# Border of stages in a two-layer trunk: the last chunk's residual by column tiles, squares summed on VectorE, the shift as two more moving columns

## The chip, the cores and the metric

One core of a Trainium2 chip (trn2). The metric is the device time of one execution in microseconds; lower is better. Engines are named as in the profile: PE is TensorE (PEld its weight loads), DVE VectorE, ACT ScalarE, POOL GpSimd, SP the engine that issues most DMAs.

## The reference

A sequence of 256 frames of width 2048 goes through two layers. Each layer is norm, mixer, residual, then norm, MLP, residual; the norm is modulated by vectors made from `c`:

```python
for layer in range(DEPTH):
    mod = jnp.einsum('bd,de->be', c_act, mod_w[layer]) + mod_b[layer]
    sh1, sc1, g1, sh2, sc2, g2 = [m[:, None, :] for m in jnp.split(mod, 6, axis=-1)]
    h = rms_norm(x, norm_mix_w[layer]) * (1.0 + sc1) + sh1
    mix = gdn_attn_mixer(h, w_in) if layer == 0 else mamba2_ssd(h, w_in)
    x = x + g1 * mix
    h = rms_norm(x, norm_mlp_w[layer]) * (1.0 + sc2) + sh2
    x = x + g2 * sq_relu_mlp(h, mlp_w1[layer], mlp_w2[layer])
```

What matters here is one step: from the last product of a stage over the residual, the mean of squares over 2048 features and its inverse root to the first product of the next stage.

## The kernel before

**Layout.** `x` lies transposed, features on partitions: four tiles of 128 x 4 x 256 (`self.x`, L1542). Weights stream in as chunks of 1 MB. `loader` (L473) DMAs a chunk to `raw`, and for each half makes `wh` (a rounded copy on ACT, L317) and `wl` (the rest, on DVE, L321), so that products of the reduced-precision float type reach full accuracy: high by high, high by low, low by high. Activations are pairs too: a unit holds high and low halves side by side, so that `wh` multiplies both in one matmul of 512 moving columns, and `wl` the high half in one of 256. There are four buffers each of `wh` and `wl`, and a new split waits until the matmuls have left its buffer.

**Order.** A framework that tracks tiles sets the waits, and a scheduler the order on each engine; some instructions are pinned (`keep_in_program_order`). Work is queued in Python: `emit` (L241) runs a chunk's matmuls after the next chunk's load was issued; small steps wait in `fast` and `bg` and are taken between matmuls.

**A stage's end.** A chunk of the output products (`c_item`, L565) has two column tiles of 128 features, ct 0 and ct 1, in one PSUM tile `pw` of 128 x 2 x 2 x 256. The last chunk (`cb` 7) runs "tile" by tile: ct 0's matmuls (low weights, then high), then ct 1's (high, then low). Afterwards `residual` (L918) adds the gated result to `x`: for each f (ct 0 and ct 1 of that chunk) two DVE operations at L925. There are three borders at which a norm follows: mixer to MLP in layer 0, layer 0 to layer 1, mixer to MLP in layer 1. At the kernel's end `residual` is followed by the output's DMAs.

**The norm's start.** `sumsq` (L809) squares `x` on ACT. Up to the third tile of `x` (`cb` < 3) the squares are added into `ss` on DVE (L833); for the last tile they, and `ss`, are summed over partitions by TensorE with a column of ones into `pm` (L823). `norm_r` (L837) makes the inverse root by Newton's method on DVE (`nv`, `rsy`, `rsn`, `rst`); `norm_bc` (L843) spreads it over the partitions with two transposes; `norm_unit` (L849) multiplies (`hf`, L862), rounds to the high half on ACT (L864) and takes the low half on DVE (L865).

**The early chunk.** To give TensorE work in the meantime, one chunk of the next stage is multiplied by the first eight features' tiles of `x` with the modulation's scale, before the root is known: `early_units` (L707) prepares units `xs`, `early_item` (L726) multiplies. The root is applied later to the product (`terms`, L733), and the shift's share comes in by 16 matmuls of the same weights with `sh` (two columns, high and low; L768) into a third PSUM tile, transposed back in `terms` (L741 to L745: `er`, `ee`, `eb`). `early_add` (L777) adds it where the next stage's first half is finished. `norm` (L872) runs the early chunk step by step among the norm's instructions, and `first_blocks` (L786) starts the next stage's first two chunks as units arrive.

Of the kernel before, what the change touches and what calls it, by code (L numbers as in the profile page):

```python
# [18 lines left out]
P = 128  # L19
# [93 lines left out]
class Trunk:  # L113
# [39 lines left out]
    def unit(self, dt=F32, shape=None):  # L153
        return self.u_p.tile(shape or [P, 4, SEQ], dt, tag="u", name=self.nm("u"))
# [410 lines left out]
    def c_item(self, ps, src, act, first, last, after=None, order="kind"):  # L565
# [5 lines left out]
        def run():  # L571
# [39 lines left out]
    def c_blocks(self, w, cbs, acts, then, r0=0, tail=False):  # L611
# [9 lines left out]
        for r in range(2):  # L621
            for cb in cbs:
                after = (lambda cb=cb: then(ps[cb], cb)) if r else None
                self.c_item((lambda cb=cb: get(cb)), w[r0 + r, cb], (lambda n, r=r: acts(4 * r + n)), r == 0, r == 1, after,
                            "tile" if tail and r else "kind")
# [61 lines left out]
    def out_blocks(self, w, acts, r0, sink, tail=True):  # L687
# [11 lines left out]
        for m, (cb, r) in enumerate(seq):  # L699
            if m == len(seq) - self.nstill0:  # L700
                self.still = self.nstill0
            after = (lambda cb=cb: sink(ps.pop(cb), cb)) if r else None
            self.c_item((lambda cb=cb: get(cb)), w[r0 + r, cb], (lambda n, r=r: acts(4 * r + n)), r == 0, r == 1, after,
                        "tile" if tail and m == len(seq) - 1 else "kind")


    def early_units(self, key):  # L707
# [6 lines left out]
        self.sh = sh = self.s_p.tile([P, 8, 2], F32R, tag="sm", name=self.nm("sh"), bufs=32)  # L714
        self.split(shift[:, :8], sh[:, :, 0], sh[:, :, 1])
        for n in range(4):
            u = self.unit(F32R, [P, 2, 2, SEQ])
            for f in range(2):
                k = 2 * n + f
                x = self.x[k // 4][:, k % 4]  # L720
                nc.scalar.activation(u[:, f, 0], x, AF.Copy, scale=scale[:, k : k + 1])
                nc.vector.scalar_tensor_tensor(u[:, f, 1], x, scale[:, k : k + 1], u[:, f, 0].bitcast(F32), op0=ALU.mult, op1=ALU.subtract)
            xs.append(u)
            yield

    def early_item(self, src):  # L726
# [4 lines left out]
        self.early = res = {}  # L731

        def terms():  # L733
            rows = self.s2([P, SEQ], tag="er")
            nc.scalar.copy(rows[:2], res["b"][:2, :SEQ])
# [4 lines left out]
            yield  # L740
            ps = self.pm([P, 2, SEQ])[:, 0, :4]  # L741
            for ct in range(2):
                self.tr(ps[:, 2 * ct : 2 * ct + 2], rows[:2, ct * P : ct * P + P], 2)
            bias = self.small(4, "eb")
            nc.scalar.copy(bias, ps)  # L745
            nc.vector.tensor_tensor(bias[:, :2], bias[:, 0:4:2], bias[:, 1:4:2], op=ALU.add)
            yield
            nc.vector.tensor_tensor(e, e, self.row(self.R, 2), op=ALU.mult)
            return e, bias

        def run():
            while self.etask and not self.etask.done:
                self.etask.step()
            xs = self.xs
            halves = self.tiles(ws, 256)
            res["b"] = b = self.pm([P, 512])
            for hf in range(2):
                for k2 in (0, 2):
                    for k in (k2, k2 + 1):
                        u = xs[2 * hf + k // 2][:, k % 2]  # L760
                        for ct in range(2):
                            self.mmx(res["p"][ct].rearrange("p a t -> p (a t)"), halves[hf][0][:, k, ct * P : ct * P + P], u.rearrange("p a t -> p (a t)"), hf == k == 0, False)
                        for ct in range(2):
# [5 lines left out]
                yield  # L769
# [5 lines left out]
        res["p"] = [self.pm([P, 2, SEQ]) for _ in range(2)]  # L775
# [33 lines left out]
    def sumsq(self, cb, b, late=False):  # L809


        sq = self.s2([P, 2, SEQ], tag="sq")
        x = self.x[cb][:, 2 * b : 2 * b + 2]
        if cb == 3:
            if b == 0:
                self.ps_r = self.pm([P, 512])[:, :2]
            for f in range(2):
                self.nc.scalar.activation(sq[:, f], x[:, f], AF.Square)

            def sums():  # L820
                for n, a in enumerate((() if b else (self.ss,)) + (sq[:, 0], sq[:, 1])):
                    for t in range(2):
                        self.mmx(self.ps_r[:, t : t + 1], a[:, t * P : t * P + P], self.ones[:, :1], b == n == t == 0, b == n == t == 1)  # L823
# [5 lines left out]
            return  # L829
        self.nc.scalar.activation(sq, x, AF.Square)  # L830
        for f in range(2):
            if not cb == b == f == 0:
                self.nc.vector.tensor_tensor(self.ss, sq[:, 0] if cb == b == 0 else self.ss, sq[:, f], op=ALU.add)  # L833
# [38 lines left out]
    def norm(self, key, srcs):  # L872
# [15 lines left out]
        next(run)  # L888
# [29 lines left out]
    def residual(self, ps, cb, key, last, final=False):  # L918
# [4 lines left out]
        for f in range(2):  # L923
# [4 lines left out]
        if last and not final:  # L928
            self.sumsq(cb // 2, b, cb == 7)
# [559 lines left out]
    def mlp(self, layer, acts, after=None):  # L1489
# [20 lines left out]
        for f in range(NF):  # L1510
# [11 lines left out]
            for cb in range(8):  # L1522
                if f == NF - 1 and cb == 6:
                    self.still = 4
                self.c_blocks(w2, (cb,), lambda n, a=a: a[n].finish(),
                              lambda ps, cb, f=f: self.residual(ps, cb, ("mlp", layer), f == NF - 1, layer == 1 and f == NF - 1), f * 2,
# [285 lines left out]
```

## Time and profile before

| | us |
|---|---|
| median of 3 runs | 2716.48 (2715.31 to 2716.92) |
| profiled execution: span (the page gives no other time for it) | 2717.6 |
| PE busy | 2665.0 (98%) |
| PEld busy | 2350.4 (86%) |
| DVE busy | 2147.6 (79%) |
| ACT busy | 1351.2 (50%) |

The span runs from the first to the last instruction. A line of the page gives a group's place in the code, engine, operation, tiles written and read, count, busy time, mean length of one in ns, and the idle time of its engine ahead of it with what ended it. A row of the timeline has start, length, engine, line, operation and count, and in brackets the idle time just before. A row of the chain of waits has start, length and what ran. A row of the windows has a stretch, its length, the busy time and count of PE, PEld, DVE, ACT and POOL, the granted TensorE clock, the share of the DMA engines and GB/s. Matmuls overlap, so their lengths are longer than the distance from one to the next.

### The profile page before, as it was taken

The numbers are of one execution on the slowest core, as the hardware profiler recorded it, in microseconds if no ns is written. First come the engines' busy times: TensorE is split into PE (matmuls) and PEld (weight loads), VectorE is DVE, ScalarE is ACT, GpSimd is POOL, SyncE is SP. The second block draws the span as 40 slices with busy tenths as digits, with TensorE's granted clock in tenths as the row PEclk, the third lists the DMA queues.
The fourth block names the chain that finished last, engine by engine and source line by source line (L and its number), as shares of the span: only waits on it lengthen the run. The fifth ranks groups of instructions, "written<-read, shape, count | busy, mean of one in ns | idle before, by whom it ended". The sixth has DMA issues, their size and how long they took to land.

```text
span 2717.6 us, 39677 instructions
## 1 busy us (share of the span) xinstructions
PE 2665.0 (98%) x15664; PEld 2350.4 (86%) x15664; DVE 2147.6 (79%) x3081; ACT 1351.2 (50%) x1976; POOL 24.5 (1%) x98
## 2 busy tenths in 40 slices
PE   5999999999999999999999999999999999999999
PEld 5887989888888888888888888888888888888888
DVE  7998998987888888889889876897777855555554
ACT  3444454546445354454556544665555354454452
POOL 1000000000000000000000000000000000000000
PEclk9999999999999999999999999999999999999999
DMA  9986487867899898988456665554558855555554
GB/s 341 353 325 235 172 301 272 294 241 282 322 339 328 328 336 330 333 331 307 165 185 217 217 234 200 203 185 172 196 177 293 324 201 188 188 191 193 186 192 134
DMA packets 100459, 680.06 MB, mean 250 GB/s; under 512 B 11185, under 2 KB 14513, under 8 KB 19377
## 3 DMA queue, kind: packets, MB, share of 16 engines
q1 hardware_dynamic: 95376, 669.07, 68.5%
q10 hardware_dynamic: 4896, 8.46, 1.0%
q8 instruction: 123, 2.02, 0.3%
q14 instruction: 64, 0.52, 0.1%
HBM read 675.33 MB, written 2.16 MB: 249 GB/s over the span
## 4 chain that ended last, share of the span: by engine, by line
PE 90%; DVE 6%; DMA 1%; ACT 1%; issue 1%; SPq 0%; ACTq 0%; DVEq 0%
PE pw L308 70%; PE pg L308 13%; PE pm L311 4%; PE pm L308 3%; DVE mraw L439 2%; DVE wl L321 1%; PE pm L314 1%; DMA mraw<-in_mod_dram 1%; DVE u L1592 0%; ACT wh L317 0%; DVE hf L862 0%; ACT pm L1042 0%; DMA raw<-in_w_ab_dram 0%; DMA x<-in_x_dram 0%; DVE u L865 0%
## 5 line engine op out<-in xcount | busy, mean ns | idle before, releaser
L317 ACT CAST wh<-raw 128x1024 fp32r<-128x1024 f32 x870 | 907.1, 1051 | 1031.6 <-PE pw L308 732.9
L321 DVE TENSOR_TENSOR wl<-raw,wh 128x1024 fp32r<-128x1024 f32 x870 | 1048.7, 1220 | 463.8 <-ACT wh L317 349.6
L308 PE MATMUL pw<-u,wh 128*128 128x512 f32 x5584 | 1321.6, 391 | 2.6 <-DVE pad L973 1.9
L308 PEld LDWEIGHTS pw<-u,wh 128*128 128x128 f32 x5584 | 1032.2, 188 | 208.2 <-issue 3.3
L308 PEld LDWEIGHTS pw<-u,wl 128*128 128x128 f32 x5584 | 702.3, 191 | 21.3 <-issue 2.1
L308 PE MATMUL pw<-u,wl 128*128 128x256 f32 x5584 | 714.5, 283 | 0.3 <-DVE wl L321 0.3
L439 DVE SCALAR_TENSOR_TENSOR mraw<-mraw,crow 128x2048 f32<-128x2048 f32 x192 | 438.0, 2283 | 17.8 <-DMA mraw<-in_mod_dram 17.5
L308 PE MATMUL pg<-wh,u 128*128 128x512 f32 x864 | 281.6, 397 | 0.0
L308 PEld LDWEIGHTS pg<-wh,u 128*128 128x128 f32 x864 | 161.9, 188 | 32.1 <-issue 0.5
L925 DVE SCALAR_TENSOR_TENSOR x<-pw,mod,x 128x256 f32<-128x256 f32 x352 | 161.1, 478 | 22.6 <-PE pw L308 20.3
L308 PE MATMUL pg<-wl,u 128*128 128x512 f32 x432 | 169.9, 393 | 0.7 <-DVE wl L321 0.5
L308 PE MATMUL pg<-u,wh 128*128 128x256 f32 x672 | 124.6, 285 | 0.0
L308 PEld LDWEIGHTS pg<-u,wh 128*128 128x128 f32 x672 | 105.7, 192 | 0.3
L308 PEld LDWEIGHTS pg<-wl,u 128*128 128x128 f32 x432 | 81.4, 188 | 17.6 <-DVE wl L321 2.1
L308 PE MATMUL pg<-u,wl 128*128 128x256 f32 x336 | 95.3, 284 | 0.0
L308 PE MATMUL pm<-u,wh 128*128 128x256 f32 (+1 forms) x304 | 64.6, 310 | 19.2 <-ACT wh L317 19.2
L308 PEld LDWEIGHTS pm<-u,wh 128*128 128x128 f32 x304 | 49.1, 198 | 20.3 <-ACT wh L317 20.0
L308 PEld LDWEIGHTS pg<-u,wl 128*128 128x128 f32 x336 | 64.4, 192 | 0.1
L984 DVE SCALAR_TENSOR_TENSOR u<-pad,cst,u 128x256 f32<-128x256 f32 x144 | 60.6, 477 | 3.3 <-ACT u L978 3.2
L864 ACT ACTIVATE u<-hf,mod 128x256 fp32r<-128x256 f32 x64 | 29.3, 502 | 53.0 <-DVE hf L862 53.0
L1504 ACT ACTIVATE rl<-rs 128x512 f32<-128x512 f32 x64 | 40.4, 632 | 18.9 <-DVE rs L1499 14.4
L308 PE MATMUL pm<-u,wl 128*128 128x256 f32 x176 | 46.1, 290 | 3.1 <-DVE wl L321 3.1
(299 smaller groups left out, 1580.5 us busy)
## 6 DMA issues: line engine op xcount, KB each, us to landing
raw<-in_w_dram SPq DMA_DIRECT2D x256, 1024.0 KB, 5.0
mraw<-in_mod_dram SPq DMA_DIRECT2D x192, 1024.0 KB, 6.0
raw<-in_w_ab_dram SPq DMA_DIRECT2D x56, 1024.0 KB, 5.7
raw<-in_w_ssd_dram SPq DMA_DIRECT2D x48, 1024.0 KB, 4.9
raw<-in_w_sz_dram SPq DMA_DIRECT2D x32, 1024.0 KB, 4.9
raw<-in_wo_ssd_dram SPq DMA_DIRECT2D x32, 1024.0 KB, 4.8
raw<-in_wo_ab_dram SPq DMA_DIRECT2D x16, 1024.0 KB, 5.2
sE<-sd_rowd ACTq DMA_DIRECT2D x32, 256.0 KB, 4.9
```

The costliest lines, as they stand in the source:

```text
L308: self.nc.tensor.matmul(o, a, b, start=start, stop=stop, skip_group_check=True)
L311: self.nc.tensor.matmul(o, lhsT, rhs, start=True, stop=True, skip_group_check=True)
L314: self.nc.tensor.transpose(o, a, self.ident[:k, :k])
L317: a = self.nc.scalar.copy(hi, src)
L321: b = self.nc.vector.tensor_tensor(lo, src, hi.bitcast(F32), op=ALU.subtract)
L439: x = nc.vector.scalar_tensor_tensor(raw, raw, 1.0, self.crow, op0=ALU.mult, op1=ALU.mult, accum_out=t[:, f : f + 1])
L864: nc.scalar.activation(hi, h[:, f], AF.Identity, bias=shift[:, col])
L925: nc.vector.scalar_tensor_tensor(x[:, 2 * b + f], ps[:, f, n], g[:, 2 * cb + f : 2 * cb + f + 1], x[:, 2 * b + f], op0=ALU.mult, op1=ALU.add)
L984: nc.vector.scalar_tensor_tensor(h, pad[:, f, 1 + q : 257 + q], w[:, q, j : j + 1], h, op0=ALU.mult, op1=ALU.add)
L1504: nc.scalar.activation(rl, lo, AF.Relu)
```

## The change

1. **Residual by column tiles.** In the last chunk of a stage, `residual` is called for f = 0 as soon as ct 0's matmuls are issued (a new argument `mid` of `c_item`), and for f = 1 after ct 1's. This holds for the last chunk of the kernel too.
2. **Squares on DVE.** For the last tile of `x`, the squares are added into `ss` on DVE as well, up to f = 0 of the last half; TensorE sums only `ss` and the last f's squares. The kernel's first norm goes the same way.
3. **Shift as columns.** The early units get two more columns behind the 256 of the high half, the shift's high and low part (copied on ACT); high and low half no longer lie side by side. The early matmuls become 258 (high) and 256 (low) columns instead of 512, and `wl` takes 258 instead of 256. The 16 shift matmuls, their PSUM tile and the transposes go. The two columns are copied out on ACT (`eb`), and the root multiplies the product straight from PSUM.

```diff
+    def unit_ext(self):
+        t = self.u_p.tile([P, 4 * SEQ + 4], F32R, tag="u", name=self.nm("u"))
+        cut = 2 * (SEQ + 2)
+        return t[:, :cut].rearrange("p (f t) -> p f t", f=2), t[:, cut:].rearrange("p (f t) -> p f t", f=2)
...
-    def c_item(self, ps, src, act, first, last, after=None, order="kind"):
+    def c_item(self, ps, src, act, first, last, after=None, order="kind", mid=None):
...
                         if len(cts) == 2 or hf:
                             yield
+                if cts == (0,) and mid:
+                    mid()
...
-            after = (lambda cb=cb: sink(ps.pop(cb), cb)) if r else None
+            tile = tail and m == len(seq) - 1
+            mid = (lambda cb=cb: sink(ps[cb], cb, (0,))) if tile else None
+            after = ((lambda cb=cb: sink(ps.pop(cb), cb, (1,))) if tile else (lambda cb=cb: sink(ps.pop(cb), cb))) if r else None
...
         for n in range(4):
-            u = self.unit(F32R, [P, 2, 2, SEQ])
+            hi, lo = self.unit_ext()
+            nc.scalar.copy(hi[:, :, SEQ:], sh[:, 2 * n : 2 * n + 2].bitcast(F32))
...
         def terms():
-            rows = self.s2([P, SEQ], tag="er")
-            nc.scalar.copy(rows[:2], res["b"][:2, :SEQ])
+            bias = self.small(4, "eb").rearrange("p (c n) -> p c n", c=2)
+            for ct in range(2):
+                nc.scalar.copy(bias[:, ct], res["p"][ct][:, SEQ:ext])
+            nc.vector.tensor_tensor(bias[:, :, 0], bias[:, :, 0], bias[:, :, 1], op=ALU.add)
+            yield
             e = self.s2([P, 2, SEQ], tag="ee")
             for ct in range(2):
-                nc.scalar.copy(e[:, ct], res["p"][ct][:, 1])
-                nc.vector.tensor_tensor(e[:, ct], res["p"][ct][:, 0], e[:, ct], op=ALU.add)
...
-            nc.vector.tensor_tensor(e, e, self.row(self.R, 2), op=ALU.mult)
-            return e, bias
+                nc.vector.tensor_tensor(e[:, ct], res["p"][ct][:, :SEQ], self.R, op=ALU.mult)
+            return e, bias[:, :, 0]
...
+                for k in range(4):
+                    hi, lo = (a[:, k % 2] for a in self.xs[2 * hf + k // 2])
+                    for n, w in enumerate(halves[hf]):
                         for ct in range(2):
-                            self.mmx(res["p"][ct][:, 1], halves[hf][1][:, k, ct * P : ct * P + P], u[:, 0], False, hf == 1 and k == 3)
+                            o, c = res["p"][ct], w[:, k, ct * P : ct * P + P]
+                            self.mmx(o[:, :ext], c, hi, hf == k == n == 0, hf == n == 1 and k == 3)
+                            if n == 0:
+                                self.mmx(o[:, :SEQ], c, lo, False, False)
                     yield
-                for k in range(4):
-                    for n in range(2):
-                        self.mmx(b[:2, :SEQ], self.sh[:, 4 * hf + k], halves[hf][n][:, k], hf == k == n == 0, hf == 1 and k == 3 and n == 1)
...
+        if cb < 3 or b == 0:
+            sq = self.s2([P, 2, SEQ], tag="sq")
+            nc.scalar.activation(sq, x, AF.Square)
+            for f in range(2):
+                if not cb == b == f == 0:
+                    nc.vector.tensor_tensor(self.ss, sq[:, 0] if cb == b == 0 else self.ss, sq[:, f], op=ALU.add)
+            return
+        for f in fs:
+            sq = self.s2([P, SEQ], tag="sq")
+            nc.scalar.activation(sq, x[:, f], AF.Square)
+            if f == 0:
+                nc.vector.tensor_tensor(self.ss, self.ss, sq, op=ALU.add)
+                continue
...
-        next(run)
+        for _ in range(3):
+            next(run)
         self.sums()
...
-        for f in range(2):
+        for f in fs:
             for n in range(2):
                 nc.vector.scalar_tensor_tensor(x[:, 2 * b + f], ps[:, f, n], g[:, 2 * cb + f : 2 * cb + f + 1], x[:, 2 * b + f], op0=ALU.mult, op1=ALU.add)
```

The order of TensorE at the middle border, from the end of ct 0 (`pw` is the last chunk's tile, `pm` the early chunk's, `u` an activation unit, `wh` and `wl` a weight chunk's parts; [waits X] names the engine waited for). Before:

```order
L308 MATMUL pw_11897<-u_11197,wh_11893 128x512 x2
L308 MATMUL pw_11897<-u_10902,wh_11889 128x512 x2
L308 MATMUL pw_11897<-u_11000,wh_11889 128x512 x2
L308 MATMUL pw_11897<-u_11099,wh_11893 128x512 x2
L308 MATMUL pw_11897<-u_11197,wh_11893 128x512 x2
L308 MATMUL pw_11897<-u_10902,wl_11890 128x256 x2
```

and now, from the row behind the end of ct 0:

```order
L317 MATMUL pm_11969<-u_11785,wh_11920 128x258 [waits Activation_49]
L317 MATMUL pm_11969<-u_11785,wh_11920 128x256
L317 MATMUL pm_11970<-u_11785,wh_11920 128x258
L317 MATMUL pm_11970<-u_11785,wh_11920 128x256
L317 MATMUL pm_11969<-u_11785,wl_11921 128x258 [waits DVE_49]
L317 MATMUL pm_11970<-u_11785,wl_11921 128x258
L317 MATMUL pm_11969<-u_11785,wh_11920 128x258
L317 MATMUL pm_11969<-u_11785,wh_11920 128x256
L317 MATMUL pm_11970<-u_11785,wh_11920 128x258
L317 MATMUL pm_11970<-u_11785,wh_11920 128x256
L317 MATMUL pm_11969<-u_11785,wl_11921 128x258
L317 MATMUL pw_11885<-u_10892,wh_11877 128x512 [waits DVE_49]
```

The first row of before is the end of ct 0. Before, ct 1 followed at once, without a wait; now its first matmul waits for DVE, whose residual reads the same PSUM tile, and 11 of the early chunk's 48 matmuls stand ahead of it.

The order of DVE at the same border (`x` is the residual, `pw` the last chunk, `wl` a weight split, `nv` the start of the root). Before:

```order
L321 TENSOR_TENSOR wl_11933<-raw_11930,wh_11932 128x1024 [waits DMAHW0_49,PE_49,Activation_49]
L321 TENSOR_TENSOR wl_11937<-raw_11930,wh_11936 128x1024 [waits PE_49,Activation_49]
L321 TENSOR_TENSOR wl_11984<-raw_11981,wh_11983 128x1024 [waits DMAHW1_49,PE_49,Activation_49]
L925 SCALAR_TENSOR_TENSOR x_82<-pw_11897,mod_128,x_82 128x256 [waits PE_49]
L925 SCALAR_TENSOR_TENSOR x_82<-pw_11897,mod_128,x_82 128x256 [waits DVE_49]
L925 SCALAR_TENSOR_TENSOR x_82<-pw_11897,mod_128,x_82 128x256
L925 SCALAR_TENSOR_TENSOR x_82<-pw_11897,mod_128,x_82 128x256 [waits DVE_49]
L838 TENSOR_SCALAR nv_12000<-pm_11878 128x2 [waits PE_49]
```

and now:

```order
L330 TENSOR_TENSOR wl_11921<-raw_11918,wh_11920 128x1024 [waits DMAHW0_49,PE_49]
L823 TENSOR_TENSOR ss<-ss,sq_11871 128x256 [waits DVE_49]
L330 TENSOR_TENSOR wl_11925<-raw_11918,wh_11924 128x1024 [waits PE_49,Activation_49]
L934 SCALAR_TENSOR_TENSOR x_82<-pw_11885,mod_128,x_82 128x256 [waits PE_49]
L934 SCALAR_TENSOR_TENSOR x_82<-pw_11885,mod_128,x_82 128x256 [waits DVE_49]
L829 TENSOR_TENSOR ss<-ss,sq_11946 128x256 [waits Activation_49]
L330 TENSOR_TENSOR wl_11974<-raw_11971,wh_11973 128x1024 [waits DMAHW1_49,PE_49,Activation_49]
L934 SCALAR_TENSOR_TENSOR x_82<-pw_11885,mod_128,x_82 128x256 [waits PE_49]
L934 SCALAR_TENSOR_TENSOR x_82<-pw_11885,mod_128,x_82 128x256 [waits DVE_49]
L846 TENSOR_SCALAR nv_12000<-pm_11994 128x2 [waits PE_49]
```

The residual's f = 0 half moved ahead of the weight split of the next chunk (`wl_11984`, now `wl_11974`); the f = 1 half still stands behind it. The two adds of squares are new.

More of the change, by code (lines that the diff above doesn't have):

```diff
@@ L622, in c_blocks @@
             for cb in cbs:
[L623 removed]
+                tile = tail and r == 1
+                mid = (lambda cb=cb: then(ps[cb], cb, (0,))) if tile else None
+                after = ((lambda cb=cb: then(ps[cb], cb, (1,))) if tile else (lambda cb=cb: then(ps[cb], cb))) if r else None
                 self.c_item((lambda cb=cb: get(cb)), w[r0 + r, cb], (lambda n, r=r: acts(4 * r + n)), r == 0, r == 1, after,
[L625 removed]
+                            "tile" if tile else "kind", mid)
     def n_item(self, src, acts, width, sink):
@@ L915, in norm, with residual @@
         return get
-    def residual(self, ps, cb, key, last, final=False):
+    def residual(self, ps, cb, key, last, final=False, fs=(0, 1)):
         nc = self.nc
```

61 lines of the change are left out of this document (20 added, 41 removed).

## Prediction

> **What bounds the kernel now.** I read the page first, then the stretch from the last matmul of a stage to the first of the next at the three borders, then the middle border instruction by instruction, then the kernel's two ends, then the granted clock.
>
> The page, parts 1 and 4: TensorE is busy for 98% of the span and makes 90% of the chain that ended last.
>
> ```profile
> PE 2665.0 (98%) x15664; PEld 2350.4 (86%) x15664; DVE 2147.6 (79%) x3081; ACT 1351.2 (50%) x1976; POOL 24.5 (1%) x98
> PE 90%; DVE 6%; DMA 1%; ACT 1%; issue 1%; SPq 0%; ACTq 0%; DVEq 0%
> ```
>
> So an edit pays where it takes TensorE work away, or where TensorE waits. The three borders, each from the start of the early chunk's first matmul to the first `pw` matmul of the next stage (columns: length, then busy time of PE, PEld, DVE, ACT, POOL; granted clock; DMA):
>
> ```profile
> 1301.54:1310.99 9.45, 9.02 (x60) 7.07 (x58) 7.33 (x23) 2.41 (x6) 0.00 (x0) 1.00 0.04 15
> 583.28:592.72 9.44, 9.00 (x61) 7.07 (x59) 7.34 (x23) 2.42 (x6) 0.00 (x0) 1.00 0.02 6
> 1995.76:2005.19 9.43, 8.98 (x60) 7.07 (x58) 7.33 (x23) 2.42 (x6) 0.00 (x0) 1.00 0.03 10
> ```
>
> They are alike: some 9.44 us, 9.0 of it busy. The early chunk covers the chain residual, squares, sums, rsqrt, broadcast, norm almost exactly. I work on the middle one. Its timeline (start, length, engine, line, instruction, count; idle before):
>
> ```profile
> 1296.93 3.82 PE L308 MATMUL pw<-u,wh 128*128 128x512 f32 x16
> 1300.58 1.12 PE L308 MATMUL pw<-u,wl 128*128 128x256 f32 x8
> 1301.31 1.22 DVE L321 TENSOR_TENSOR wl<-raw,wh 128x1024 fp32r<-128x1024 f32 x1 [3.69 <-ACT wh L317]
> 1301.54 0.63 PE L308 MATMUL pm<-u,wh 128*128 128x512 f32 x2
> 1302.45 1.91 DVE L925 SCALAR_TENSOR_TENSOR x<-pw,mod,x 128x256 f32<-128x256 f32 x4
> 1304.40 0.42 ACT L818 ACTIVATE sq<-x 128x256 f32<-128x256 f32 x1 [0.49 <-DVE x L925]
> 1305.56 0.50 PE L308 MATMUL pm<-ones,sq 128*128 128x1 f32 x4
> 1305.92 0.28 PE L308 MATMUL pm<-wl,sh 128*2 128x256 f32 x1
> 1306.04 0.28 PE L308 MATMUL pm<-wh,sh 128*2 128x256 f32 x1
> 1306.10 0.16 DVE L838 TENSOR_SCALAR nv<-pm 128x2 f32<-128x2 f32 x1 [1.74 <-PE pm L308]
> 1308.37 0.40 PE L314 MATMUL pm<-ident,rsy 128*128 128x128 f32 x2 [0.32 <-DVE rsy L276]
> 1310.99 1.20 PE L308 MATMUL pw<-u,wh 128*128 128x512 f32 x4
> ```
>
> Matmuls are pipelined, so their price is the step from start to start: 16 of 512 columns take 1300.58 - 1296.93 = 3.65 us, 0.229 each; 8 of 256 columns 1301.54 - 1300.58 = 0.96, 0.12 each (0.115 net, half of 0.229). The two shift matmuls are 0.12 apart.
>
> **The change part by part.** *Sums moved off TensorE.* The chain of waits shows what one ones-product with its two halves costs ahead of the last column tile:
>
> ```profile
> 1289.20 0.34 PE pm L308 x4
> 1291.70 0.34 PE pm L308 x4
> 1294.25 0.34 PE pm L308 x4
> ```
>
> Three of these go at each border; TensorE does not wait there, so this is 3 x 0.34 = 1.02 us each. The VectorE adds that replace them (0.42 us each) fall where VectorE was idle, 3.69 us ahead of 1301.31 alone.
>
> *Shift as columns.* The early chunk was 16 x 0.229 + 16 x 0.115 + 16 shift matmuls x 0.115 = 7.3 us and becomes 48 x 0.116 (16 of 256 columns, 32 of 258) = 5.6. The trace has no 258-column matmul; the nearest rows lie on one line (256 at 0.115, 512 at 0.229), so 258 should be 0.116. The saving of 1.8 us is cover, not path, unless TensorE is what ends the border. That has to be worked out.
>
> *Residual by column tiles.* Before, ct 0 ends 8 x 0.229 after 1296.93, at 1298.76, and VectorE starts at 1302.45, behind a weight split that waits for its buffer (1301.31). After, the f = 0 half starts when ct 0 drains (0.17 later), takes half of 1.91, and ends some 1.2 us after ct 0. But the order shows that the ct 1 matmuls now wait for it, and that 11 early matmuls stand ahead of them: 11 x 0.116 = 1.27 us. So TensorE loses nothing there, and ct 1 ends 1.27 us later with 37 early matmuls (4.3 us) left instead of the whole chunk.
>
> From the end of ct 1 (T): the weight split still stands ahead of the f = 1 residual, which so starts at T + 0.91 as before (1302.45 - 1301.54), takes 0.95, squares 0.42: ready at T + 2.35. The sums stand behind 19 early matmuls and the `ss` product: 19 x 0.116 + 0.34 = T + 2.54, so TensorE's queue sets them; `nv` follows 0.54 later (1306.10 - 1305.56), at T + 3.08. From `nv` to the first `pw` it was 1310.99 - 1306.10 = 4.89, made of rsqrt, broadcast, a pinned weight split, norm:
>
> ```profile
> 1308.06 0.04 DVE rsy L276
> 1308.14 1.23 DVE wl L321
> 1309.37 1.18 DVE hf L862 x3
> 1310.54 0.41 DVE u L865
> ```
>
> None of that is edited. First `pw` at T + 7.97, against 9.45 before, less 1.27 for the fill: 0.21 us gained. With the sums 1.23 us a border, 3.7 us in all. And TensorE is out of early work at about T + 5.8: it now waits 0.35 us for the broadcast and 2.1 us for the norm. The stall that was covered is late next.
>
> *The terms.* The four small copies (`er`, `ee`, `eb`) become two ahead of the norm's activations, in ACT's wait for `hf`. At the end of the first blocks TensorE waited for `er`:
>
> ```profile
> 1326.03 1.22 DVE L321 TENSOR_TENSOR wl<-raw,wh 128x1024 fp32r<-128x1024 f32 x1
> 1327.16 0.87 DVE L865 SCALAR_TENSOR_TENSOR u<-hf,mod,u 128x256 fp32r<-128x256 f32 x2
> 1327.55 0.28 PE L314 MATMUL pm<-ident,er 2*128 2x2 f32 x2 [0.61 <-ACT er L735]
> ```
>
> 0.61 + 0.21 us go, but the next matmuls in line now want the last unit's low half, done 0.45 us after 1327.16, and then a weight split that moved behind it (1.22 us). I get 0.6 + 0.2 + 0.2 us of waits for them: nothing gained, -0.4 to +0.4.
>
> *The kernel's two ends.* At the start TensorE's sums gate the first modulation products:
>
> ```profile
> 10.44 0.43 DVE ss L833
> 11.01 4.41 PE pm L308 x20
> 15.44 0.17 DVE nv L838
> 15.92 2.30 DVE mraw L439 x2
> ```
>
> 20 records at 0.22 become 8 (1.76 us) behind three more adds (3 x 0.45): 15.44 becomes 14.15, 1.3 us gained, and VectorE sets the pace from there. At the end there is no early work for the fill:
>
> ```profile
> 2712.72 1.92 DVE L925 SCALAR_TENSOR_TENSOR x<-pw,mod,x 128x256 f32<-128x256 f32 x4 [7.77 <-PE pw L308]
> ```
>
> TensorE stands 1.2 us for the f = 0 residual, and half of the 1.92 us at the end goes: 0.2 to 0.3 us lost.
>
> *The granted clock.* The new gaps have a price of their own. Here it fell in stretches of 3.41 us; the stretch before each, and one that did not fall:
>
> ```profile
> 86.60:90.01 3.41, 1.87 (x9) 1.21 (x7) 2.83 (x7) 1.32 (x2) 0.00 (x0) 1.00 0.93 320
> 90.01:93.43 3.42, 2.73 (x20) 2.52 (x21) 3.27 (x4) 3.42 (x7) 0.00 (x0) 1.00 0.58 232
> 424.52:427.93 3.41, 1.40 (x12) 1.21 (x11) 3.27 (x12) 0.81 (x1) 0.00 (x0) 0.99 0.78 257
> 427.93:431.34 3.41, 3.40 (x17) 3.41 (x18) 2.17 (x4) 1.65 (x3) 0.00 (x0) 0.51 0.94 360
> 1376.84:1380.25 3.41, 1.50 (x7) 0.99 (x6) 3.34 (x9) 2.46 (x5) 0.00 (x0) 0.99 0.43 183
> 1380.25:1383.66 3.41, 3.41 (x10) 2.67 (x9) 3.41 (x11) 0.89 (x3) 0.00 (x0) 0.51 0.44 127
> ```
>
> 1380.25 - 427.93 is 279 x 3.413: the stretches lie on a fixed grid. One with 1.40 or 1.50 us busy is followed by half clock, one with 1.87 is not. The cost:
>
> ```profile
> 1374.08 3.82 PE L308 MATMUL pw<-u,wh 128*128 128x512 f32 x16
> 1379.80 5.48 PE L308 MATMUL pw<-u,wh 128*128 128x512 f32 x16 [1.91 <-DVE pad L973]
> ```
>
> 5.48 - 3.82 = 1.66 us. A new gap of 0.35 + 2.1 us idle exceeds the 1.54 to 1.91 us that decide, if it falls into one stretch. With the limit in the middle (1.7) that holds for 2.46 us of the 3.41 at which a stretch can begin: 72% at each border, 61% and 81% with the limit at its ends. So I expect two of three borders to lose 1.6 us each.
>
> The Trainium skill, TensorE: Matmul & The Clock Gate, "HAM oscillation", has the clock fall only after idle gaps of more than about 3.4 us. The trace differs: it fell after 1.91 us, and the measurement decides; by that rule the clock would hold at all three borders, the first rival below.
>
> *The sum*, from the profiled execution: its span is 2717.6 us (the page gives no time around it), 1.1 above the median of the runs, 2716.48. Gains 1.3 (start) + 3.7 (borders) - 0.2 (end) = 4.8; clock 2 x 1.6 = 3.2 back; net 1.6 us. From the median: 2714.9 us. With all three borders slowed 2716.5, with one 2713.3.
>
> **The rivals.**
>
> *Clock holds.* For: the 1.71 us idle in the stretch at 86.60 cost nothing, and the gap may straddle two stretches. Against: both gaps of 1.9 us and more did. Time: 2716.5 - 4.8 = 2711.7, by my terms' uncertainty 2711.0 to 2712.5.
>
> *TensorE work is the path.* If the f = 1 residual came ahead of the weight split or the sums earlier in the queue, the border would end with TensorE's work: 3 x (1.02 + 1.8 + 0.8) + 1.3 = 12.2 us, 2704.3. Against: the order has both where they were.
>
> *258 columns are dear (slower).* If the two extra columns double a step, 20 of them stand between the end of ct 0 and the sums (7 in the fill, 13 behind ct 1): 2.3 us, and some 12 before the broadcast add 0.9 beyond their 0.5 us of slack. 3 x 3.2 = 9.6 us against 4.8 gained: 2721.3. It decides from 0.06 us extra on a 258-column step. Against: 256 and 512 lie on one line.
>
> *The change doesn't do what it says*: that the tile-wise residual does not run beside ct 1 but ahead of it is in my sum already; if the fill also failed to cover it (early weights late), each border loses up to 1.27 us more: about 2718.
>
> **How the numbers follow.** Forecast (two or three borders slowed) 0.57; clock holds, or falls once, 0.25; TensorE is the path 0.05; dear 258 columns 0.06; fill fails or an unseen reordering 0.07. About 0.2%, 5.4 us, is what a measurement of this kernel can tell from no change. Faster by more: TensorE's path, and a fifth of the held-clock case: 0.10. Slower by more: the 258 case and a little: 0.07. Else 0.83. The range takes in the held clock's lower bound, 2711.0, and up to 2717.4, one border's loss above no change; it leaves out some 0.18.
>
> **What would show it.** Right: first `pw` 8.0 us after the last ct 1 matmul at each border, with a PE wait of about 2 us on DVE `u`; 11 early matmuls and no wait ahead of ct 1; granted clock near 0.5 for 3.4 us after most borders; `nv` of the start near 14.15; a PE wait of 1.2 us on DVE `x` at the end. Wrong: a border gap filled, 258-column steps over 0.13 us, or a clock of 1.00 after gaps of 2 us.

## The result and the profile after

The changed kernel takes 2733.67 us (median of 5 runs, 2731.72 to 2735.84), the kernel before in the same comparison 2715.49 us: ratio 1.0069, 95% interval 1.0057 to 1.0082. It is slower by some 18 us, where 1.6 us less was forecast, and lies far outside the range (2711.0 to 2717.4).

Where did it go? TensorE's line on the page after, and two groups of its matmuls (busy time, mean length of one in ns, idle before):

```profile
PE 2675.1 (98%) x15610; PEld 2332.6 (85%) x15610; DVE 2152.1 (79%) x3090; ACT 1350.1 (49%) x1978; POOL 24.2 (1%) x98
L317 PE MATMUL pw<-u,wh 128*128 128x512 f32 x5584 | 1348.3, 396 | 10.5 <-DVE u L873 7.2
L317 PE MATMUL pw<-u,wl 128*128 128x256 f32 x5584 | 706.7, 282 | 1.2 <-DVE wl L330 0.7
```

The same groups in the kernel before:

```profile
L308 PE MATMUL pw<-u,wh 128*128 128x512 f32 x5584 | 1321.6, 391 | 2.6 <-DVE pad L973 1.9
L308 PE MATMUL pw<-u,wl 128*128 128x256 f32 x5584 | 714.5, 283 | 0.3 <-DVE wl L321 0.3
```

TensorE has 54 matmuls fewer and is busy 10 us longer. Nothing of that is at the borders: matmuls that the change does not touch, the same 5,584 of them, became longer, those of 512 columns by 5 ns; those of 256 became 1 ns shorter. The timeline in the middle of the first MLP, far from any border, shows the same from start to start. Before (start, length, count at the end):

```profile
803.67 4.00 PE L308 MATMUL pw<-u,wl 128*128 128x256 f32 x32
807.50 7.44 PE L308 MATMUL pw<-u,wh 128*128 128x512 f32 x32
814.78 4.00 PE L308 MATMUL pw<-u,wl 128*128 128x256 f32 x32
```

and after:

```profile
804.75 3.95 PE L317 MATMUL pw<-u,wl 128*128 128x256 f32 x32
808.54 7.61 PE L317 MATMUL pw<-u,wh 128*128 128x512 f32 x32
815.99 3.95 PE L317 MATMUL pw<-u,wl 128*128 128x256 f32 x32
```

32 steps of 512 columns took 814.78 - 807.50 = 7.28 us (227.5 ns each) and take 7.45 (232.8); 32 of 256 columns took 3.83 (119.7) and take 3.79 (118.4). Over a whole trace I took the mean distance from the start of such a matmul to the next start, over the 6,880 of 512 columns and the 6,592 of 256 (`pw` and `pg` tiles; the 2% and 1% of the distances that are over 300 and 160 ns, at waits and at other matmuls in between, are left out): 227.91 and 119.68 ns before, 232.38 and 118.18 after. That is 6,880 x 4.47 = 30.8 us more and 6,592 x 1.50 = 9.9 us less, 20.9 us net. It explains more than the whole loss, and leaves -2.7 us for what the prediction summed.

The borders themselves went much as forecast. The three stretches that answer to those shown of before, from the first early matmul behind ct 1 to the first `pw`:

```profile
581.35:589.60 8.25, 5.91 (x49) 5.54 (x48) 6.56 (x21) 2.40 (x7) 0.00 (x0) 1.00 0.02 8
1307.74:1315.97 8.23, 5.89 (x49) 5.51 (x48) 6.57 (x21) 2.41 (x7) 0.00 (x0) 1.00 0.00 0
2006.03:2014.28 8.25, 5.94 (x50) 5.57 (x48) 6.56 (x21) 2.39 (x7) 0.00 (x0) 0.98 0.01 2
```

8.24 us instead of 9.44. The middle one in the chain of waits (11 early matmuls, ct 1, then early ones and the sums in a row):

```profile
1303.74 1.31 PE pm L317 x11
1305.05 2.86 PE pw L317 x16
1307.91 3.05 PE pm L317 x27
```

in the timeline:

```profile
1309.73 0.64 PE L317 MATMUL pm<-u,wh 128*128 128x258 f32 x4
1310.21 0.40 PE L317 MATMUL pm<-u,wl 128*128 128x258 f32 x2
1310.44 0.50 PE L317 MATMUL pm<-ones,sq 128*128 128x1 f32 x4
...
1315.97 1.17 PE L317 MATMUL pw<-u,wh 128*128 128x512 f32 x4 [2.26 <-DVE u L873]
```

and the waits of TensorE that the change made (total, times, longest):

```profile
PE pw L317 <- DVE u L873: 7.2, 4, 2.3
PE pw L317 <- DVE x L934: 1.1, 1, 1.1
```

The reader sees the six matmuls of 258 and 256 columns between 1309.73 and 1310.44 at 0.118 us each, and the new wait of 2.26 us for the norm.

### The profile page after: what moved, and what is told of

Same layout as the page of the kernel before. It is cut to its first block, busy times and chain, and to the rows that moved or that the text cites. A ratio compares the mean times of both kernels' runs of the same rounds, so it can differ in the third digit from the quotient of the medians.

```text
span 2733.8 us, 39574 instructions
## 1 busy us (share of the span) xinstructions
PE 2675.1 (98%) x15610; PEld 2332.6 (85%) x15610; DVE 2152.1 (79%) x3090; ACT 1350.1 (49%) x1978; POOL 24.2 (1%) x98
## 4 chain that ended last, share of the span: by engine, by line
PE 89%; DVE 7%; DMA 2%; ACT 1%; issue 1%; SPq 0%; POOL 0%; DVEq 0%; ACTq 0%; POOLq 0%
PE pw L317 69%; PE pg L317 13%; PE pm L320 4%; PE pm L317 2%; DVE mraw L448 2%; DVE wl L330 2%; PE pm L323 1%; DMA mraw<-in_mod_dram 1%; DVE hf L870 0%; DVE u L873 0%; DVE u L1601 0%; DMA u<-in_attn_rel_bias_dram 0%; ACT wh L326 0%; DMA raw<-in_w_ab_dram 0%; ACT pm L1051 0%
## 5 line engine op out<-in xcount | busy, mean ns | idle before, releaser
L317 PE MATMUL pw<-u,wh 128*128 128x512 f32 x5584 | 1348.3, 396 | 10.5 <-DVE u L873 7.2
L317 PEld LDWEIGHTS pw<-u,wl 128*128 128x128 f32 x5584 | 695.0, 189 | 26.0 <-issue 2.1
L317 PE MATMUL pw<-u,wl 128*128 128x256 f32 x5584 | 706.7, 282 | 1.2 <-DVE wl L330 0.7
L317 PE MATMUL pm<-u,wl 128*128 128x256 f32 (+1 forms) x176 | 47.2, 291 | 2.9 <-DVE wl L330 2.9
```

What stands on the lines that cost most here:

```text
L317: self.nc.tensor.matmul(o, a, b, start=start, stop=stop, skip_group_check=True)
```

## The experiments

What in the change can touch matmuls all over the program? One line that the excerpt of the diff above leaves out: `unit` too now takes a tile of `[P, 4 * SEQ + 4]`, since units and extended units share a pool of 18 buffers. 4096 B per partition became 4112, a buffer 4128, so that unit n starts 4128 n and no longer 4096 n bytes behind the first. The eight weight buffers of 4096 B each lie just ahead of the units and do not move: before, every unit lay a multiple of 4096 B from every weight tile, now unit n lies 32 n B past such a place. So Theory A: the address of the units sets the step. Rival B: something else in the changed program does.

**The size alone.** The kernel before, with that tile:

```diff
-        return self.u_p.tile(shape or [P, 4, SEQ], dt, tag="u", name=self.nm("u"))
+        t = self.u_p.tile([P, 4 * SEQ + 4], dt, tag="u", name=self.nm("u"))
+        shape = shape or [P, 4, SEQ]
+        names = "abcd"[: len(shape) - 1]
+        return t[:, : 4 * SEQ].rearrange(f"p ({' '.join(names)}) -> p {' '.join(names)}", **dict(zip(names, shape[1:])))
```

> The kernel before, with the unit tile alone enlarged from 4096 to 4112 B per partition (a slot of 4128 B), nothing else of the change. Theory A (the address of a unit sets the step of the 512-column matmuls): the step goes from 227 to about 232 ns and that of the 256-column ones from 120 to 118 to 119 ns, as in the kernel after; 6,880 steps x 3.9 ns less 7,000 x 1.2 ns is some 18.5 us, so 2734 us (2731 to 2737). Rival B (something else in the changed program slows TensorE, and the size of the tile is nothing): 227 and 120 ns, 2715.5 us (2713 to 2718).

2735.18 us (2733.95 to 2737.49), ratio 1.0071 (1.0059 to 1.0084). Steps 232.37 and 118.17 ns. B falls: nothing of the change but the tile's size is needed for the whole loss. (With this size the order on TensorE differs from before in 12 of 15,664 places; with 4160 B, below, in none, and the loss is there too.)

**What about the address?** Three kernels: the changed one and the one before with a tile of 4160 B, and the one before with all units moved by 32 B at the old stride:

```diff
-        t = self.u_p.tile([P, 4 * SEQ + 4], dt, tag="u", name=self.nm("u"))
+        t = self.u_p.tile([P, 4 * SEQ + 16], dt, tag="u", name=self.nm("u"))
```

```diff
+        pool("pd0", 1).tile([P, 8], F32, tag="pd0", name="pd0")
         self.u_p = pool("up", 18)
+        pool("pd1", 1).tile([P, 8], F32, tag="pd1", name="pd1")
```

> The kernel after with the unit tile padded to 4160 B per partition, so that every unit starts at a multiple of 64 B as all did before. Theory A1 (the start of a unit within 64 B matters): steps back at 227 and 120 ns, and what is left is the change as the prediction summed it, 2714.9 us (2711 to 2717.4). Theory A2 (the stride of the units matters, that they no longer lie 4096 B apart): steps as in the kernel after, about 2734 us. Rival B (the changed program): about 2734 us.

> The kernel before with the unit tile padded to 4160 B per partition: a multiple of 64 B, and no longer 4096 B apart. Theory A1: 2715.5 us, steps 227 and 120 ns. Theory A2 (the stride of 4096 B matters): about 2734 us, steps 232 and 118 ns. Rival B: 2715.5 us.

> The kernel before with all 18 units moved by 32 B (stride 4096 B kept, everything behind them again at a multiple of 64 B). Theory A1 (the start within 64 B): all units are off now, where in the kernel after every second one is, so at least the loss of the kernel after, 2734 us, and up to twice it, 2753 us. Theory A2 (the stride): 2715.5 us. Rival B: 2715.5 us.

2730.28 us (1.0051; 1.0037 to 1.0065), 2731.32 (1.0059; 1.0046 to 1.0072) and 2732.25 (1.0062; 1.0050 to 1.0075). So both sub-theories fall: multiples of 64 B do not help (A1), and keeping the stride of 4096 B does not either (A2). In the third the steps are another pair again, and the same throughout:

```profile
804.86 3.90 PE L310 MATMUL pw<-u,wl 128*128 128x256 f32 x32
808.60 7.63 PE L310 MATMUL pw<-u,wh 128*128 128x512 f32 x32
816.06 3.89 PE L310 MATMUL pw<-u,wl 128*128 128x256 f32 x32
```

512 columns went up to 233.1 ns (7.46 / 32), 256 columns down to 116.9 (3.74 / 32). What all three slow kernels have in common is that most units and the weights no longer lie at the same place within 512 B (with 4160 B all but units 0, 8 and 16).

**Own place, or place relative to the weights?** Weights and units moved together, and a bare kernel of nothing but matmuls (its loop last):

```diff
+        pool("pd0", 1).tile([P, 8], F32, tag="pd0", name="pd0")
         self.w_p = pool("wp", 4)
         self.u_p = pool("up", 18)
+        pool("pd1", 1).tile([P, 120], F32, tag="pd1", name="pd1")
```

```python
        for n in range(96):
            k, ct = n // 2 % 4, n % 2
            a = wt[:, s // 4 + k * 256 + ct * P : s // 4 + k * 256 + ct * P + P]
            b = mv[:, m // 4 + k * 1024 : m // 4 + k * 1024 + c]
            nc.tensor.matmul(o[:, :c], a, b, start=n == 0, stop=n == 95, skip_group_check=True)
```

> The kernel before with the weights' tiles and the units all moved by 32 B, so that they stand to each other as before. Theory R (relative place): 227 and 120 ns, 2715 us. Theory M (the moving operand's own start): 233 and 117 ns as with the units alone moved, 2732 us.

> A bare kernel that computes nothing of the reference: runs of 96 matmuls of 512 and of 256 fp32r columns with nothing beside them, the moving and the stationary operand so many bytes past a multiple of 512 B. Theory R (the place of the moving operand relative to the stationary ones counts): (0,0) steps 227 and 120 ns, (32,0) about 233 and 117 as in the shifted kernel, (32,32) and (64,64) back at 227 and 120. Theory M (the start of the moving operand alone counts): (32,0) and (32,32) both 233 and 117, (0,32) 227 and 120. Theory D (VectorE and ScalarE collide with TensorE in SBUF, and the address decides how): 227 and 120 ns in every case, since both are idle here.

2715.82 us, ratio 0.9998 (0.9990 to 1.0007): with both at 32 B the loss is gone. The bare kernel's chain of waits (start, length; the name says columns, bytes of the moving operand past 512, bytes of the stationary one; 96 matmuls each):

```profile
25.93 21.76 PE c512m0s0y L45 x96
47.69 11.51 PE c256m0s0y L45 x96
59.20 22.40 PE c512m32s0z L45 x96
81.60 11.20 PE c256m32s0z L45 x96
114.78 10.88 PE c256m64s0z L45 x96
260.95 21.78 PE c512m256s0z L45 x96
428.69 21.76 PE c512m32s32z L45 x96
450.45 11.51 PE c256m32s32z L45 x96
461.96 22.39 PE c512m0s32z L45 x96
```

21.76 / 96 = 226.7 ns at distance 0, wherever the two lie; 22.40 / 96 = 233.3 at 32 B either way round; 256 B is as good as 0 for 512 columns. For 256 columns distance 0 is among the worst (119.9) and 32 better (116.7). These are the steps of the whole kernels, with VectorE and ScalarE idle: theories M and D fall, R stands. What collides inside no run shows.

**The change with units where they were.** The extended high halves go into the convolution's padding buffers and two more like them:

```diff
+    def unit_ext(self, n):
+        hi = self.s_p.tile([P, 2, 260], F32R, tag="pad" if n < 2 else "xh", name=self.nm("xh"), bufs=2)
+        return hi[:, :, : SEQ + 2], self.unit(F32R)[:, :2]
```

> The whole change with the units back at 4096 B: the two extended tiles of an early unit's high half lie in the convolution's padding buffers and two more such buffers, the low half in a unit. If the size of the unit was all that went wrong: steps 227 and 120 ns and the prediction's sum, 2714.9 us (2711 to 2717.4), with 7.97 us from the last matmul of column tile 1 to the first pw of the next stage. If the change itself costs (258 columns, sums on VectorE): above 2717.4 us.

2712.07 us (2710.81 to 2715.28, 11 runs), ratio 0.9990 (0.9981 to 0.9999); steps 227.96 and 119.69. From ct 1 to the first `pw` 8.23 us at each border (1296.52 to 1304.75 at the middle one). The change as such is a small gain, within the range forecast (by which terms, see below).

**Can the distance be used?** If 256 columns run better at another distance, the low weights alone could lie there, since those matmuls load `wl`. Moved by 32 B:

```diff
         self.w_p = pool("wp", 4)
+        pool("pd0", 1).tile([P, 8], F32, tag="pd0", name="pd0")
+        self.wl_p = pool("wlp", 4)
+        pool("pd1", 1).tile([P, 120], F32, tag="pd1", name="pd1")
...
-                wl = self.w_p.tile([P, 1024], F32R, tag="wl", name=self.nm("wl"))
+                wl = self.wl_p.tile([P, 1024], F32R, tag="wl", name=self.nm("wl"))
```

> The kernel before with only the low halves of the weights (wl) moved by 32 B; units and high halves stay. Theory R: the 256-column matmuls, which load wl, go from 120 to 117 ns, 5,920 x 3.3 ns = 19.5 us less, the 432 that stream wl by 512 columns 6 ns more each, 2.6 us: 2715 - 17 = 2698 us. Theory M: only those 432 change, 2718 us, or nothing, 2715 us.

2715.90 us, ratio 1.0000 (0.9992 to 1.0009). A miss of my own making: `wl` 32 B up puts the unit 32 B *below* it, a distance of 480, where the bare kernel showed 118.4 ns. Steps were 229.29 and 118.28: 9.5 us lost on the 512 columns, 9.2 won on the 256. It does not speak against R. At a distance of 64 B (112 and 16 words in place of 8 and 120), after a finer look at the bare steps:

> The bare kernel again (it computes nothing of the reference), the stationary operands at multiples of 512 B and the moving one at finer distances. Theory R (TensorE's reads of the moving and of the next stationary operand meet in SBUF, and their distance decides how often): the step depends on the distance in pieces of 16 or 32 B; it goes up by whole clock cycles spread over a pattern that repeats, the means lie between 226.7 and 234 ns for 512 columns and 113 and 120 ns for 256, and 64 gives about 229 and 113 again, as in the first such run. Theory S (that a few addresses are special by chance of the order of the runs): 64 no longer gives 113 ns when other distances come before it.

> The kernel before with only the low halves of the weights moved, by 448 B, so that a unit lies 64 B past them (modulo 512 B), the distance at which 256 columns took 113.3 ns by themselves; high halves and units stay. Theory R: 5,920 matmuls of 256 columns go from 120 to 113.3 ns, -39.5 us; the 432 that stream wl by 512 columns go from 227 to 233 ns, +2.8 us; where the two kinds alternate some 4 us are lost again, as 32 B showed (512-column steps from 228.5 to 229.0 ns, others 2 to 3 ns more): 2683 us (2678 to 2690). If the distance counted only in a bare loop, where VectorE, ScalarE and the DMA are idle: 2715.5 us.

> The whole change with units of 4096 B and with the low halves of the weights moved by 448 B. Theory R: the gain of both, 2712.1 - 32 = 2680 us (2674 to 2687). If the distance counted only in a bare loop: 2712 us.

2709.12 us, ratio 0.9975 (0.9966 to 0.9985), and with the change 2704.05, 0.9958 (0.9945 to 0.9970). Gains, but the first is a fifth of what was expected: the step in the program is 117.7 ns and not 113.3. The second bare kernel shows that step too; its row at 64 B:

```profile
249.97 11.31 PE c256m64s0z L44 x96
```

256 columns at 64 B, 10.88 / 96 = 113.3 ns in the first bare kernel, took 117.8 in this one (S). The other distances of this one gave 229.1 to 236.6 ns for 512 columns, none as good as 0. So the same distance has more than one step. Does what ran before decide?

> The bare kernel a third time (it computes nothing of the reference): 96 matmuls of 256 columns at a distance of 64, 112, 448 or 32 B from the stationary operands, each after 40 matmuls of six other kinds (512 columns at 64, 0, 32 and 112 B, 256 columns at 0 and 32 B). Theory H (the step is a pattern into which the two streams of reads fall, and which of several depends on what ran before): at one distance the mean differs by what came before, 113.3 ns after some and 117.8 after others, at 64 B at the least. Theory F (the step is a function of the distance alone): each distance has one mean, after whatever.

The chain of the third bare kernel (256 columns, distance, letter of the 40 matmuls that ran just before: a 512 columns at 64 B, b 512 at 0, c 256 at 0):

```profile
34.98 10.88 PE t64aftera L45 x96
55.01 10.90 PE t112aftera L45 x96
75.08 11.31 PE t448aftera L45 x96
115.86 11.31 PE t64afterb L45 x96
136.27 10.92 PE t112afterb L45 x96
224.50 10.90 PE t448afterc L45 x96
```

10.88 us (113.3 ns) at 64 B behind a, 11.31 (117.8) behind b and the four others; at 448 B and at 32 B it also takes two values. F falls, and of H this much is shown: one distance has several steps, and the starts settle into one of them and keep it (at 64 B the first 24 and the last 24 of the 96 have the same mean, 113.3 behind a and 117.8 behind b). That the kind of work just before decides is not shown: 512 columns at 64 B stood just ahead of 256 at 64 B in all three bare kernels, and these took 113.3, 117.8 and 113.3 ns. Only 112 B stayed at 113.3 to 114.0 ns behind all six. Three whole kernels at other distances (120 and 8 words; 16 and 112; and `wl` in a pool behind all others, 16 B into tiles of 1152 words):

> The whole change with units of 4096 B, the low halves of the weights moved by 480 B, so that a unit lies 32 B past them. With all units moved by 32 B, 256 columns took 117.2 ns on the mean in the whole program, against 118.3 at a distance of 64 B: 5,920 x 1.1 = 6.5 us less than that kernel, 2697.5 us (2694 to 2703). If 512-column steps suffer as at +32 B (229.0 ns, pg 2 to 3 ns more), 1 to 3 us of that are lost. If low halves do nothing more: 2704 us.

> The whole change with units of 4096 B, the low halves of the weights moved by 64 B (distance 448 B), at which the first bare run showed 113.4 ns and which no second one has repeated. If that holds in the program: 5,920 x 5 = 30 us less than at 64 B, 2675 us. Theory H (another pattern, as at 64 B): 117 to 119 ns, 2704 us, give or take 5.

> The whole change with units of 4096 B, the low halves of the weights at 400 B past a multiple of 512, so that a unit lies 112 B past them: the one distance at which 256 columns reached 113.3 ns in the bare kernel after all six kinds of predecessor (means of 113.3 to 114.0 ns over 96). If the program falls into the same pattern: 5,920 x (118.3 - 114) = 25 us less than at 64 B, 2679 us (2674 to 2690). If it falls into another, as it did at 448 B: 2700 to 2706 us. The lows are in a pool behind all others, which changes nothing in any engine's order.

2701.17 us, ratio 0.9947 (0.9933 to 0.9961); 2704.73, 0.9955 (0.9942 to 0.9968); 2714.50, 0.9995 (0.9987 to 1.0004). The first has the lowest median of the study, within the range expected, though its interval overlaps those of the kernels with `wl` at 448 and at 64 B; its steps in the MLP:

```profile
807.14 3.90 PE L316 MATMUL pw<-u,wl 128*128 128x256 f32 x32
810.87 7.45 PE L316 MATMUL pw<-u,wh 128*128 128x512 f32 x32
818.16 3.90 PE L316 MATMUL pw<-u,wl 128*128 128x256 f32 x32
```

7.29 / 32 = 227.8 and 3.73 / 32 = 116.6 ns: high halves at distance 0, low halves at 32. The last, at 112 B, is a miss: (824.72 - 820.90) / 32 = 119.4 ns in the program, 113.3 to 114.0 in the bare loop.

```profile
813.61 7.45 PE L315 MATMUL pw<-u,wh 128*128 128x512 f32 x32
820.90 3.99 PE L315 MATMUL pw<-u,wl 128*128 128x256 f32 x32
824.72 1.55 PE L315 MATMUL pw<-u,wh 128*128 128x512 f32 x6
```

A bare loop does not foretell the pattern of a program. Why it differs here stays open; the order in which units and weights follow each other, or the other engines, could each do it.

All whole kernels together (distance of the units from the stationary weights modulo 512 B; mean steps; their sum over 6,880 and 6,592 matmuls against before; measured difference of medians):

| kernel | distance | 512, 256 columns, ns | by the steps, us | measured, us |
|---|---|---|---|---|
| before | 0 | 227.91, 119.68 | | |
| tile 4112 alone | 32 n | 232.37, 118.17 | +20.7 | +20.2 |
| changed kernel | 32 n | 232.38, 118.18 | +20.9 | +18.2 |
| before, tile 4160 | 64 n | 231.42, 118.39 | +15.6 | +16.3 |
| changed, tile 4160 | 64 n | 231.46, 118.41 | +16.1 | +15.3 |
| units + 32 B | 32 | 233.22, 116.76 | +17.3 | +17.2 |
| units and weights + 32 B | 0 | 227.94, 119.68 | +0.2 | +0.2 |
| `wl` + 32 B | 0, `wl` 480 | 229.29, 118.28 | +0.3 | +0.3 |
| `wl` + 448 B | 0, `wl` 64 | 228.60, 117.67 | -8.5 | -6.9 |
| changed, tile 4096 | 0 | 227.96, 119.69 | +0.4 | -3.6 |
| the same, `wl` + 448 B | 0, `wl` 64 | 228.61, 117.73 | -8.0 | -12.0 |
| the same, `wl` + 480 B | 0, `wl` 32 | 228.84, 116.84 | -12.3 | -14.8 |
| the same, `wl` + 64 B | 0, `wl` 448 | 228.55, 117.67 | -8.8 | -11.2 |
| the same, `wl` at 400 B | 0, `wl` 112 | 228.83, 119.06 | +2.2 | -1.0 |

Where the change is absent the steps give the measured time within 1.6 us; where it is in, the rest is -2.7, -0.8, -4.0, -4.0, -2.5, -2.4 and -3.2, on the mean -2.8 us.

## Why the prediction was wrong

**The step that failed** is the sum, "Gains 1.3 (start) + 3.7 (borders) - 0.2 (end) = 4.8; clock 2 x 1.6 = 3.2 back": it priced "Shift as columns" by the early matmuls and the copies, and held that the rest of the program stays as it was. The tile that holds two more columns moved the start of 17 of 18 units, and the step of 13,472 matmuls with it: +20.7 us by the steps, +20.2 measured with the size alone. No rival had it; the one on the slower side, dear 258 columns, is a different mechanism, and it falls: 0.118 us a step in the rows above and 0.123 on the mean of 19, where it needed 0.06 us extra on 0.116.

**Point by point, the rest.**

- *Border.* Forecast 7.97 us from ct 1 to the first `pw`, measured 8.24: the sums come 2.70 us after T (1310.44 - 1307.74) instead of 2.54, since the 19 steps ahead of them took 0.123 us each on the mean and not 0.116, and from `nv` to the first `pw` it took 4.99 for 4.89. With 1.3 us of fill (11 matmuls from 1303.74 on, 1.31 in the chain) that border term, 0.21 us gained, is 0.1 lost. The 1.02 us of sums ahead of ct 1 are gone as forecast.
- *The new stall.* 2.1 us for the norm forecast, 2.26 to 2.3 measured; of the 0.35 us for the broadcast 0.1 is left (8.23 - 5.89 us idle in all). 1.2 forecast for f = 0 at the kernel's end, 1.1 measured, once; so at the borders the fill covered it, as forecast. Behind the last matmul `x` is ready after 1.04 us, 1.96 before: the end loses 0.2 us, as forecast.
- *The start.* `nv` at 14.61 us, 14.15 forecast, 15.44 before. But in the seven traces with the old sums it stood at 14.09 (tile 4112 alone) to 15.70 (units and weights + 32 B), with a median of 15.44, and in the seven with the new at 14.41 to 14.96, median 14.95. That is 0.5 us of the 1.3 forecast, and less than the spread; how large the term is stays open.
- *The terms.* Nothing was forecast, -0.4 to +0.4. From the first `pw` behind a border to the 201st, a stretch that before held the wait for `er`, it took 35.90 to 35.93 us at the three borders before (starts counted in the traces). With the change and tiles of 4096 B it took 35.85 at the first border and 35.41 at the third, where the clock did not fall; at the middle border the changed kernel has 35.65 and tile 4112 alone 36.06. So 0.1, 0.4 and 0.5 us are won, 1.0 in all.
- *The clock.* This was the boldest term, and it held in kind. Stretches of the changed kernel at the first border and the middle one, on the grid of 3.413 us:

```profile
587.18:590.59 3.41, 1.15 (x6) 0.86 (x5) 3.41 (x8) 2.44 (x6) 0.00 (x0) 1.00 0.01 2
590.59:594.01 3.42, 3.42 (x13) 3.01 (x12) 3.42 (x8) 1.93 (x5) 0.00 (x0) 0.50 0.44 120
1314.24:1317.65 3.41, 1.68 (x9) 1.53 (x10) 3.41 (x8) 2.91 (x6) 0.00 (x0) 1.00 0.02 5
1317.65:1321.06 3.41, 3.41 (x20) 2.91 (x19) 3.41 (x10) 1.31 (x3) 0.00 (x0) 1.00 0.62 199
```

  2.26 us idle in a stretch: half clock in the next. 1.73 idle, because the gap lay across two stretches: no fall. Over the seven kernels that have the change it fell at 15 of 21 borders, 71%, where 72% was forecast; in seven that have not, at none. That the two shares lie so close is partly luck: the gap was 2.26 us and not 2.46, and the limit at these borders lay between 1.85 and 1.90 us and not at 1.7, with which the forecast's own working gives some 57%. The first rival, that the clock holds, was wrong as a rule; of the "1.71 us idle in the stretch at 86.60" on which it leans, only 3.41 - 1.87 = 1.54 lay in that stretch. The price, from the chain of the changed kernel with tiles of 4096 B, after the first border (no fall) and the middle one (fall):

```profile
587.87 13.38 PE pw L313 x75
...
1304.75 14.10 PE pw L313 x70
```

  14.10 - 70 x 13.38 / 75 = 1.6 us by the mean of rows that mix two lengths. Matmul by matmul, the order being the same, the 65th starts 11.27 us behind the first without a fall and 12.79 with one: 1.5 us, forecast 1.6.
- *The sum without the size.* -1.6 us forecast, -3.6 measured (0.9990; 0.9981 to 0.9999), -2.8 on the mean of the seven. The parts as measured give 3 x 1.02 (sums) - 3 x 0.1 (border) - 0.2 (end) + 1.0 (terms) - 1.5 x 15 / 7 (clock) = +0.3, next to nothing. Two things stand beside them: the start, 0.5 by the medians, and the old gap that ends at 1379.80 in the kernel before, after which the clock fell in 5 of 7 traces without the change and in 2 of 7 with it, 1.5 x 3 / 7 = 0.6 us. That makes a gain of 1.4; the other 1.4 us are not explained. (Falls near 428 us, in 2 of 7 traces without the change and none with it, and near 90 us, in none and 3 of 7, are not counted.) So it is partly luck that the time without the size lies in the range: the forecast sum had more of the start and of the border, and nothing for the terms and the old gap. One such difference is not known better than to some 2.5 us (the interval of the -3.6 runs from -5.2 to -0.3).

## What to carry to other kernels

Before a tile in a shared pool is made a few bytes larger, look at where every other tile of that pool and behind it starts then; here 16 B cost 20 us in matmuls that the edit does not name, while everything it does name was worth 3. Read the step of a matmul, start to start, away from the edit first: if it moved, the cause is not in the edited stage. Keep operands that stream against each other at the same place within 512 B unless a measurement in the whole program shows another distance to be better.

## What the runs showed of the hardware that I had not expected

- The step of matmuls in the reduced-precision float type (fp32r in the rows) depends on the distance of moving and stationary operand in SBUF, modulo 512 B: 226.7 ns for 512 columns at 0 and 226.9 at 256 B, 229 to 237 at the others tried; 119.9 ns for 256 columns at 0, 113.3 to 120.8 elsewhere, with VectorE and ScalarE idle. The Trainium skill, SBUF — State Buffer, section "SBUF: two separate sides", says that contention on the engines' side comes from the port pair that GpSimd and VectorE share alone, and that "PE, ACT, and DVE's dedicated pair never wait on anyone". Taken strictly, an address would by that rule not change a step of TensorE with the other engines idle; 22.40 us against 21.76 for the same 96 matmuls does not agree, and the measurement decides. (The rule is on one engine against another; whether TensorE's reads of its two operands meet, no run shows.) The section "Operand start alignment" of that page of the Trainium skill is, in its own words, "about legality, not speed"; here units that start 32 B further on cost 17 us.
- One distance can have several steps: 256 columns at 64 B ran at 113.3 or 117.8 ns for 96 matmuls on end; what chooses between them is not shown.
- The clock falls for 3.41 us when TensorE was idle for long enough within one stretch of a fixed grid, and at the borders the limit is sharper than the prediction had it. In the changed kernel with tiles of 4096 B, at the first border and the middle one:

```profile
586.02:589.43 3.41, 1.56 (x9) 1.41 (x10) 3.41 (x8) 2.85 (x6) 0.00 (x0) 1.00 0.01 2
...
1302.82:1306.23 3.41, 1.48 (x9) 1.33 (x9) 3.41 (x8) 2.77 (x6) 0.00 (x0) 1.00 0.00 0
1306.23:1309.65 3.42, 3.42 (x13) 2.84 (x12) 3.42 (x9) 1.45 (x4) 0.00 (x0) 0.50 0.58 180
```

  1.85 us idle held, 1.93 fell; of the 21 borders the 6 at which it held had at most 1.85 us in any stretch, the 15 at which it fell 1.90 to 2.33. Elsewhere the idle time alone does not settle it: near 87 us the clock fell after 1.71 (the same with `wl` + 64 B), 1.76 (the kernel above) and 1.80 us idle (changed, tile 4160), and held after 1.72 (units and weights + 32 B). Behind the first 60 us of all 14 traces it fell after every stretch with 1.87 us idle or more and after none with 1.66 or less.
